# Row sums of 64 MB on one core: the first seven blocks' results get a store of their own

## Chip, cores, metric

One core of one Trainium2 chip. The metric is the device time of one execution in microseconds (us), lower is better. The kernel before takes 162.84 us (median of 3 runs, 162.84 to 163.09).

## The reference

```python
batch, seq, dim = 32, 512, 1024          # x: float32, 67.11 MB
def reference(x, multiplier):            # multiplier = 0.5
    return (np.sum(x, axis=-1) * multiplier).astype(np.float32)   # 16,384 results, 64 KB
```

## The kernel before

The 16,384 rows are laid over 128 partitions, 128 consecutive rows each. Eight blocks of 16 rows per partition (8 MB each) stream through three buffers. VectorE sums eight rows of a block in one instruction, ScalarE the other eight one by one. The last block arrives in five smaller pieces, so that little work is left after the last byte. All results collect in one tile, `res`, and leave in one store. All DMAs, loads and store, are issued by SyncE (SP), on one queue.

```python
x_rows = x_flat.rearrange("(p c) d -> p c d", p=P)
out_view = out.rearrange("b s -> (b s)").rearrange("(p c) -> p c", p=P)   # 128 rows of 512 B
...
for b in range(n_blocks - 1):                    # seven blocks of 8 MB
    t = x_pool.tile([P, B, D], fp32, name="xb")  # bufs=3
    loads.append(nc.sync.dma_start(out=t, in_=x_rows[:, c0 : c0 + B, :]))
    nc.vector.reduce_sum(...)                    # rows 0 to 7 of the block
    nc.vector.tensor_single_scalar(out=res[...], ...)   # times 0.5
    for r in range(h, B): act_row(t, r, c0 + r)  # rows 8 to 15
...
# last block: pieces of 8, 5, 2 rows, then row 15 in two parts (640 and 384 columns)
dve_span(t, B - 1, 0, cut, part)
dve_span(t, B - 1, cut, D, res[:, rows - 1 : rows], start=part)

seen = nc.sync.nop()                             # SP waits here for the loads and ScalarE
for i in loads[-8:] + acts[-1:]:
    tc.add_manual_dep(seen.ins, i.ins.name, ...)
store = nc.sync.dma_start(out=out_view, in_=res)
...
nc.at_finalize(start_loads_at_entry)  # moves the loads that wait for nothing (three) ahead of the entry barrier
```

## Time and profile before

| | before |
|---|---|
| time, median of 3 | 162.84 us |
| span of the profiled run | 161.1 us |
| read from HBM | 67.11 MB, 417 GB/s over the span |
| VectorE, ScalarE busy | 42% each |
| chain of waits | 86% loads, 11% VectorE |
| last VectorE work ends, last store issued, landed | 158.68, 158.78, about 160.3 us |

From the page of the kernel before: the span, the DMA engines' busy tenths in 40 equal slices (9 is 90% or more; a slice of 4.0 us holds only one or two of the blocks' 64 KB packets, which take 2.43 us each in the trace, and this is probably why 7 and 9 alternate), the queue's packets, megabytes and share of 16 engines' span, and the chain that ended last, by engine and then by line.

```profile
span 161.1 us, 233 instructions
...
DMA  7997997997997997997997998998998998999990
...
q1 hardware_dynamic: 1872, 67.18, 96.9%
...
DMA 86%; DVE 11%; SPq 1%; issue 0%; DVEq 0%
DMA xb<-in_x_dram 86%; DVE sums L76 11%; SPq L94 1%; DVE xb L60 1%; SPq L74 0%; DVE part L60 0%; DVEq L188 0%
...
```

The loads take 96.9% of all DMA time there is, and 86% of the chain. From the table of windows of the same kernel (stretch, its length, then each engine's busy time and instruction count, the clock, the DMA share and GB/s):

```profile
...
148.00:150.00 2.00, 1.61 (x5) 1.66 (x3) 0.00 (x0) 1.00 0.98 420
150.00:152.00 2.00, 0.92 (x4) 2.00 (x5) 0.00 (x0) 1.00 0.98 420
159.00:160.00 1.00, 0.00 (x0) 0.00 (x0) 0.00 (x0) 1.00 0.23 66
...
```

From 148 to 152 us the queue is full at 420 GB/s. Between 159 and 160 us only the store moves: 0.23 of that microsecond on the average engine. The timeline of the kernel before (start, duration, engine, line, operation, operands, and in brackets the idle time before it and what ended it), cut to VectorE's start on block seven and to the tail:

```profile
...
138.56 8.69 DVE L76 TENSOR_REDUCE sums<-xb 128x8 f32<-128x8192 f32 x1 [10.46 <-DMA xb<-in_x_dram]
...
157.68 0.49 DVE L60 CUSTOM_DVE_ANT_0 xb<-xb 128x320 f32<-128x320 f32 x1
...
158.26 0.42 DVE L60 CUSTOM_DVE_ANT_0 xb<-xb,part 128x192 f32<-128x192 f32 x1
...
158.78 0.35 SPq L123 DMA_DIRECT2D out_dram<-res  x1
```

The last row's first piece starts at 157.68, VectorE ends at 158.26 + 0.42 = 158.68, and SyncE issues the store 0.10 us later. The list of DMA issues of the same kernel (destination, source, queue, operation, count, size, us from issue to landing; the 192 KB are the last row's second part), and SyncE's waits after 145 us (who, for whom, us in total, times, longest):

```profile
...
xb<-in_x_dram SPq DMA_DIRECT2D x1, 192.0 KB, 47.6
...
out_dram<-res SPq DMA_DIRECT2D x1, 64.0 KB, 1.6
```

```profile
...
SPq L115 <- DMA xb<-in_x_dram: 38.9, 1, 38.9
SPq L188 <- DMA out_dram<-res: 1.2, 1, 1.2
...
```

The last load was issued at 110.49. The store needs 1.6 us to land; after it has landed there is only the exit. SyncE has nothing to do in most of the last 42 us: 38.9 us of them is one wait for loads.

### The profile page before, as it was taken

To read this page: it belongs to the slowest core of one execution; us is meant where nothing else is said; L and a number is where in the kernel's file an instruction comes from. 1 tells how busy PE (TensorE), PEld (TensorE's weight loads), DVE (VectorE), ACT (ScalarE), POOL (GpSimd) and SP (SyncE) were. 2 spreads that over 40 slices of the span, in tenths; PEclk is the share of its full clock that TensorE was granted. 3 is DMA by queue.
4 is the path that set the end of the run, shared out by engine and by line. 5 is a ranking of instruction groups with operands and counts; after the bars stand their busy time and mean duration, and the time that the engine had idled before them with its cause. 6 is when DMAs were issued, how large, how long until landed. Compare 5 with 4: busy or idle time off the path is not lost.

```text
span 161.1 us, 233 instructions
## 1 busy us (share of the span) xinstructions
DVE 68.1 (42%) x34; ACT 67.9 (42%) x127; POOL 0.2 (0%) x4
## 2 busy tenths in 40 slices
DVE  0000049700695008930099102990049700697453
ACT  3000049600694008920099001980039700596862
POOL 0000000000000000000000000000000000000000
DMA  7997997997997997997997998998998998999990
GB/s 260 521 456 325 521 456 325 521 456 325 521 456 325 521 456 325 521 439 342 521 439 344 521 423 358 521 423 358 521 407 374 521 407 374 415 439 411 423 381 30
DMA packets 1873, 67.18 MB, mean 417 GB/s; under 512 B 208, under 2 KB 464, under 8 KB 592
## 3 DMA queue, kind: packets, MB, share of 16 engines
q1 hardware_dynamic: 1872, 67.18, 96.9%
q14 instruction: 1, 0.01, 0.0%
HBM read 67.11 MB, written 0.07 MB: 417 GB/s over the span
## 4 chain that ended last, share of the span: by engine, by line
DMA 86%; DVE 11%; SPq 1%; issue 0%; DVEq 0%
DMA xb<-in_x_dram 86%; DVE sums L76 11%; SPq L94 1%; DVE xb L60 1%; SPq L74 0%; DVE part L60 0%; DVEq L188 0%
## 5 line engine op out<-in xcount | busy, mean ns | idle before, releaser
L50 ACT ACTIVATE xb<-xb 128x1024 f32<-128x1024 f32 x63 | 65.6, 1043 | 88.4 <-DMA xb<-in_x_dram 88.4
L76 DVE TENSOR_REDUCE sums<-xb 128x8 f32<-128x8192 f32 x7 | 60.8, 8686 | 85.2 <-DMA xb<-in_x_dram 85.2
L50 ACT ACTIVATION_READ_ACCUMULATOR xb<-xb 128x1 f32 x63 | 11.8, 187 | 0.0
L60 DVE CUSTOM_DVE_ANT_0 xb<-xb 128x512 f32<-128x512 f32 (+1 forms) x9 | 5.6, 667 | 5.1 <-DMA xb<-in_x_dram 4.9
L50 ACT ACT_TABLE_LOAD x1 | 1.3, 1283 | 1.7 <-PEq L174 1.7
L79 DVE TENSOR_SCALAR res<-sums 128x8 f32<-128x8 f32 x7 | 1.2, 172 | 0.2
L60 DVE DVE_READ_ACCUMULATOR2_ANT res<- 128x1 f32 x9 | 0.7, 82 | 0.0
L60 DVE CUSTOM_DVE_ANT_0 xb<-xb,part 128x192 f32<-128x192 f32 x1 | 0.4, 418 | 0.1
L174 POOL MEMSET const-bfloat16-1.0<- 128x1 bf16 x1 | 0.1, 101 | 0.0
L174 POOL MEMSET const-uint8-127<- 128x1 uint8 x1 | 0.1, 101 | 0.0
L174 POOL MEMSET const-float32-0.0<- 128x1 f32 x1 | 0.1, 98 | 0.2 <-issue 0.2
L174 POOL MEMSET const-float32-1.0<- 128x1 f32 x1 | 0.1, 98 | 0.0
L60 DVE DVE_READ_ACCUMULATOR2_ANT part<- 128x1 f32 x1 | 0.1, 81 | 0.0
## 6 DMA issues: line engine op xcount, KB each, us to landing
xb<-in_x_dram SPq DMA_DIRECT2D x1, 4096.0 KB, 39.6
xb<-in_x_dram SPq DMA_DIRECT2D x1, 2560.0 KB, 45.4
xb<-in_x_dram SPq DMA_DIRECT2D x1, 1024.0 KB, 47.4
xb<-in_x_dram SPq DMA_DIRECT2D x1, 320.0 KB, 47.7
xb<-in_x_dram SPq DMA_DIRECT2D x1, 192.0 KB, 47.6
xb<-in_x_dram SPq DMA_DIRECT2D x7, 49.3
out_dram<-res SPq DMA_DIRECT2D x1, 64.0 KB, 1.6
```

The lines of the kernel that those rows point to most:

```text
L50: acts.append(nc.scalar.activation(out=t[:, r, :], in_=t[:, r, :], func=mybir.ActivationFunctionType.Copy, scale=mul, accum_out=res[:, col ...
L60: nc.vector.tensor_tensor_reduce(out=t[:, r, lo:mid], in0=t[:, r, lo:mid], in1=t[:, r, mid:hi], scale=mul, scalar=start, op0=ADD, op1=ADD, ...
L76: nc.vector.reduce_sum(out=sums[:, c0 : c0 + h], in_=t[:, 0:h, :], axis=mybir.AxisListType.X)
L79: nc.vector.tensor_single_scalar(out=res[:, c0 : c0 + h], in_=sums[:, c0 : c0 + h], scalar=mul, op=mybir.AluOpType.mult,)
L94: nc.sync.dma_start(out=t[:, lo:hi, :], in_=x_rows[:, c0 + lo : c0 + hi, :])
L174: nc = _bacc.Bacc("TRN2", target_bir_lowering=False, num_devices=1)
```

## The change

Intent: most of the 64 KB of results are ready long before the end. Send them early, under the last loads, so that the store which stands on the critical path carries only the last block's 8 KB. The description of the change names also "three leading loads in front of the entry barrier"; the kernel before has that already, and the diff doesn't touch it. The built programs confirm it: both hold three loads ahead of the barrier.

```diff
@@ after the last load is issued
+    c1 = c0                                                        # 112 = 7 blocks x 16
+    nc.sync.dma_start(out=out_view[:, 0:c1], in_=res[:, 0:c1])     # 128 rows of 448 B
     on_act = {4, 5, 6, 7, 11, 12, 14}
...
-    store = nc.sync.dma_start(out=out_view, in_=res)               # 128 rows of 512 B
+    store = nc.sync.dma_start(out=out_view[:, c1:], in_=res[:, c1:])   # 128 rows of 64 B
```

What the diff doesn't show: the DMAs carry eight completion semaphores in turn (numbers 99, 100 and 103 to 108). With one more DMA ahead of it, the last store carries 106, which block six's load had, in place of 105. Of the loads' semaphores, SyncE's waits on the line of that store name 99 before, and 99, 100 and 106 after: one semaphore instruction more. It stands behind VectorE's last result.

## The prediction

> **What bounds it.** The loads. In the page's DMA line the 16 engines are 0.9 or busier in nearly every pair of slices and move 417 GB/s on average (67.11 MB read in a span of 161.1 us); the queue's packets take 96.9% of 16 engines' span. The chain of waits is 86% DMA xb<-in_x_dram. The table of windows gives 420 GB/s at a DMA share of 0.98 between 148 and 152 us, so no queue time is free before about 157 us.
>
> Outside the stream is the tail, from the timeline: last load seen at 157.65, two VectorE pieces (0.49 and 0.42 us) to 158.68, the store issued at 158.78 (0.35 us of SyncE), landing 1.6 us after issue, about 160.4, then some 0.7 us of exit barrier to 161.1.
>
> **What the change does.** The three leading loads already stand in front of the entry barrier in the kernel before and stay there; no load changes place. What is new is one store: 57,344 bytes of results (128 rows of 448 B) go out on the same SyncE queue after the last load was issued, and the final store shrinks from 64 KB to 8 KB (128 rows of 64 B). The early store waits for VectorE and ScalarE to finish block seven, at 147.45 us (timeline); SyncE is then idle (it waits 38.9 us for loads, in SyncE's list of waits). Its issue should cost about 0.35 us, as the old store's did, hidden.
>
> **Does it delay the loads?** It is queued at about 147.8 behind loads issued by 110.9. [...] This trace has no store in flight with loads. [...]
>
> **What it gains.** Bytes of the last store. The old store occupies 0.23 of the engines in one microsecond (159 to 160, table of windows), 0.23 us on average per engine. The new one has the same 128 rows, only shorter, so at most about 0.15 us of that goes, and the rest of the 1.6 us to landing is fixed. [...] The built program has also one more semaphore wait on SyncE before the final store (a few tens of ns), and the exit waits for two stores. The final store doesn't wait for the early one.
>
> **Sum.** -0.15 to +0.4 us on 162.84: 162.9 us. Range 162.5 to 163.5. Chances: faster by over 2% 0.01, within 2% 0.98, slower by over 2% 0.01.
>
> **What would show it.** Right: early store issued near 147.5 us on SyncE with about 10 us or more to landing; the last load still at 157.6 to 157.8; VectorE's end within 0.2 us of 158.68; final store to landing 1.4 to 1.9 us. Wrong: early store landing within 2 to 3 us (it overtook the loads); the last load later than 158; the final store over 2 us.
>
> **What would make it wrong.** [...] the small early packets share engines with the loads and delay the last one by a microsecond; or the exit waiting for the early store.

The sum came to -0.15 to +0.4 us, so 162.9 us. Two terms of it are cut above, because no trace showed them: a delay of the loads by the early store, and a loss with the shorter rows. They are what led up to +0.4. What is left of the sum is the gain of at most 0.15 us, the author's estimate from the 0.23 us in the table of windows, and the extra wait of a few tens of ns. The runs below measured 0.14 us for the one (the landing, 1.558 to 1.414 us) and 62 ns for the other (e2, e6).

## The result

| | before | after |
|---|---|---|
| median, same rounds | 162.88 us (6 runs, 162.78 to 163.21) | 162.81 us (6 runs, 162.63 to 163.12) |
| ratio after/before | | 0.9994, 95% interval 0.998 to 1.0007: same |

A ratio is the mean time of one kernel's fast runs over that of the other's in the same rounds, so it is not quite the ratio of the medians. Here it can't be told from 1. The profile shows what happened beneath that. The page of the changed kernel:

```profile
span 160.9 us, 236 instructions
...
DMA  7997997998998998998998998998998998999991
...
q1 hardware_dynamic: 2016, 67.18, 97.2%
...
DMA 86%; DVE 11%; SPq 1%; issue 0%; DVEq 0%
DMA xb<-in_x_dram 86%; DVE sums L76 11%; SPq L94 1%; DVE xb L60 1%; SPq L74 0%; DVE part L60 0%; DVEq L190 0%
...
```

The 0.2 us of span is not the change's: VectorE's start on block seven, before the early store exists, is already 0.21 us earlier (138.35 against 138.56) in the timeline of the changed kernel:

```profile
...
138.35 8.69 DVE L76 TENSOR_REDUCE sums<-xb 128x8 f32<-128x8192 f32 x1 [10.46 <-DMA xb<-in_x_dram]
...
147.31 0.35 SPq L105 DMA_DIRECT2D out_dram<-res  x1
...
157.46 0.49 DVE L60 CUSTOM_DVE_ANT_0 xb<-xb 128x320 f32<-128x320 f32 x1
...
158.04 0.42 DVE L60 CUSTOM_DVE_ANT_0 xb<-xb,part 128x192 f32<-128x192 f32 x1
...
158.62 0.34 SPq L125 DMA_DIRECT2D out_dram<-res  x1
```

The early store is issued at 147.31. From block seven's start to the start on the last row's first piece it is 157.46 - 138.35 = 19.11 us, against 157.68 - 138.56 = 19.12 before: the early store does not delay the load of that piece.

That load is not the last one, though the prediction and the expectations call it so (they took 157.65 us from the chain of waits). The last row's second part lands about 0.5 us later, at 158.1 us before and at 157.9 (110.31 + 47.6) after, and in all ten traces of this document VectorE starts on it 0.13 us after its landing, so it too sets the end. From block seven's start to the start on this part it is 158.26 - 138.56 = 19.70 us before and 158.04 - 138.35 = 19.69 after: no delay there either.

VectorE ends at 158.46, and now 0.16 us pass before the store is issued, not 0.10. The changed kernel's DMA issues and SyncE's waits:

```profile
...
xb<-in_x_dram SPq DMA_DIRECT2D x1, 192.0 KB, 47.6
...
out_dram<-res SPq DMA_DIRECT2D x1, 56.0 KB, 10.8
out_dram<-res SPq DMA_DIRECT2D x1, 8.0 KB, 1.4
```

```profile
...
SPq L105 <- DVE res L79: 36.5, 1, 36.5
SPq L117 <- DMA xb<-in_x_dram: 10.1, 1, 10.1
SPq L190 <- DMA out_dram<-res: 1.1, 1, 1.1
...
```

The early store lands 10.8 us after issue, at about 158.1, ahead of VectorE's end. The last store lands in 1.4 us, not 1.6. SyncE, which had only loads to wait for, now waits 36.5 us for the results of block seven (up to 147.31), issues the early store, and then waits 10.1 us for loads: the issue is hidden in idle time. The table of windows shows the shorter store:

```profile
...
148.00:150.00 2.00, 1.82 (x5) 1.86 (x3) 0.00 (x0) 1.00 1.02 440
150.00:152.00 2.00, 0.72 (x4) 2.00 (x5) 0.00 (x0) 1.00 0.91 389
159.00:160.00 1.00, 0.00 (x0) 0.00 (x0) 0.00 (x0) 1.00 0.09 8
...
```

Between 159 and 160 us the average engine is busy for 0.09 us, not 0.23. In the stretches before, 148 to 152, the mean rate is 414 GB/s ((440 + 389) / 2) against 420; the loads' packets of that stretch (20 KB, 0.76 us each in both traces) probably fall unevenly into windows of 2 us, and the 19.11 us above, which is the better measure, shows no loss.

**The sum.** The time of the profiled run less the moment when VectorE ends is 162.93 - 158.68 = 4.25 us before and 162.63 - 158.46 = 4.17 after. So the change is worth about 0.08 us in its only place, a shorter store less a longer way to it. Read from the trace to the nanosecond (it records the start, length and size of every DMA packet, too): the landing is 0.14 us shorter (1.558 to 1.414), the way to the issue 0.06 longer, and the exit after the landing 0.01 longer (0.80 to 0.81; all runs with two or more stores have 0.81, the three with one have 0.80). The first packet of the last store starts 0.84 to 0.85 us after the issue in both traces; moving the packets takes 0.36 us before and 0.21 after, so the whole gain lies in moving them. It is far below the scatter of the load stream (0.6 us between two traces of the changed kernel, e5).

### The profile page after: what moved, and what is told of

Its sections match the earlier page's. It is cut to its first block, busy times and chain, and to the rows that moved or that the text cites. A ratio compares the mean times of both kernels' runs of the same rounds, so it can differ in the third digit from the quotient of the medians.

```text
span 160.9 us, 236 instructions
## 1 busy us (share of the span) xinstructions
DVE 68.1 (42%) x34; ACT 67.8 (42%) x127; POOL 0.2 (0%) x4
## 4 chain that ended last, share of the span: by engine, by line
DMA 86%; DVE 11%; SPq 1%; issue 0%; DVEq 0%
DMA xb<-in_x_dram 86%; DVE sums L76 11%; SPq L94 1%; DVE xb L60 1%; SPq L74 0%; DVE part L60 0%; DVEq L190 0%
## 6 DMA issues: line engine op xcount, KB each, us to landing
xb<-in_x_dram SPq DMA_DIRECT2D x1, 192.0 KB, 47.6
out_dram<-res SPq DMA_DIRECT2D x1, 56.0 KB, 10.8
```

## Experiments

Two theories. *Tail*: the early store is free; the last store is 0.13 to 0.2 us shorter; the extra wait costs 0.06; nothing else changes. *Contention*: the gain is larger, but the early store's packets (or its small rows) delay the last loads and eat it. Each run leaves one trace. All traces are read for the same figures:

- **stream**: from VectorE's start on block seven to its start on the last row's first piece. A store that delays the loads up to that piece lengthens this.
- **to last part**: the same, to VectorE's start on the last row's second part, which the last load of all sets.
- **gap**: from VectorE's end to the issue of the last store.
- **landing**: from that issue to its landing.
- **tail**: the profiled run's time less VectorE's end.

All in us, taken from the nanoseconds of the traces and then rounded, so that the last digit can differ by one from a sum of printed lines:

| run | stream | to last part | gap | landing | tail | time of the profiled run | median, runs |
|---|---|---|---|---|---|---|---|
| before | 19.12 | 19.70 | 0.10 | 1.56 | 4.25 | 162.93 | 162.88, 6 |
| after | 19.11 | 19.70 | 0.16 | 1.41 | 4.17 | 162.63 | 162.81, 6 |
| e1: no early store | 19.12 | 19.69 | 0.10 | 1.43 | 4.12 | 162.88 | 162.93, 6 |
| e2: early store, full last store | 19.10 | 19.69 | 0.22 | 1.55 | 4.37 | 163.25 | 163.10, 5 |
| e3: early store from ScalarE | 19.23 | 19.81 | 0.16 | 1.42 | 4.18 | 163.06 | 162.98, 5 |
| e4: a store per block | 19.13 | 19.78 | 0.16 | 1.43 | 4.19 | 163.08 | 163.08, 5 |
| e5: changed kernel again | 19.13 | 19.70 | 0.16 | 1.41 | 4.17 | 163.26 | 162.89, 6 |
| e6: the extra wait moved | 19.10 | 19.69 | 0.10 | 1.41 | 4.11 | 162.98 | 162.91, 6 |
| e7: changed, loads not leading | 19.10 | 19.69 | 0.16 | 1.41 | 4.16 | 163.65 | 163.68, 6 |
| e8: before, loads not leading | 19.10 | 19.70 | 0.10 | 1.56 | 4.25 | 163.75 | 163.82, 5 |

The kernel before had a median of 162.89 us (11 runs) in the rounds of e1 to e4 and 162.95 (11 runs) in those of e5 to e8; the two sets of rounds ran on two different chips.

### e1: without the early store

```diff
-    nc.sync.dma_start(out=out_view[:, 0:c1], in_=res[:, 0:c1])
```

> The early store is left out, so seven blocks of results are never written: wrong on purpose. Tail theory (the early store costs nothing, the small last store gains 0.2 us, its extra wait loses 0.06): last load landing within the scatter of the two traces (157.4 to 157.7), VectorE's end to the store's issue back to 0.10 us from 0.16, landing 1.4 us after issue, 162.6 to 162.8 us. Contention theory (the early store delays the last loads and hides part of the gain): the last load lands 0.2 us or more earlier than with the early store and the time falls to 162.5 or less.

The result was wrong, as meant. Ratio to before 1.0002 (0.9987 to 1.0017). The timeline of this run:

```profile
...
138.65 8.69 DVE L76 TENSOR_REDUCE sums<-xb 128x8 f32<-128x8192 f32 x1 [10.46 <-DMA xb<-in_x_dram]
...
157.77 0.49 DVE L60 CUSTOM_DVE_ANT_0 xb<-xb 128x320 f32<-128x320 f32 x1
...
158.34 0.42 DVE L60 CUSTOM_DVE_ANT_0 xb<-xb,part 128x192 f32<-128x192 f32 x1
...
158.86 0.35 SPq L124 DMA_DIRECT2D out_dram<-res  x1
```

The stream is 157.77 - 138.65 = 19.12 us, no shorter than with the early store (19.11), and to the last part it is 19.69 (19.70 with it): contention is out. The tail is 4.12: the small store alone saves 0.13 us of 4.25, with the gap unchanged at 0.10, and the landing is 0.13 us shorter too (1.43 against 1.56). The last row's first piece started at 157.77, 0.31 later than with the early store, so the expectation's "within 157.4 to 157.7" missed: absolute times drift by more than that from run to run (0.62 us between the two traces of the changed kernel), differences within a trace don't (a stream of 19.10 to 19.13 us in nine of ten). The median, 162.93, is above the range expected, for the same reason.

### e2: early store kept, last store full again

```diff
-    store = nc.sync.dma_start(out=out_view[:, c1:], in_=res[:, c1:])
+    store = nc.sync.dma_start(out=out_view, in_=res)
```

> The early store stays, and the last store writes all 512 B rows again, as before; it now waits for the early one to land. Tail theory: landing back to 1.6 us after issue, two more waits than before ahead of the last issue (VectorE's end to issue about 0.2 us), time 162.9 to 163.1 us; the early store has landed by 158.2, before VectorE ends, so its wait adds nothing. Contention theory: last load after 157.9, time 163.2 or more.

Correct; ratio 1.0005 (0.9992 to 1.0018). The two stores overlap, so the last one waits for the early one, and two waits more than before stand ahead of the issue. The timeline of this run:

```profile
...
158.46 0.42 DVE L60 CUSTOM_DVE_ANT_0 xb<-xb,part 128x192 f32<-128x192 f32 x1
...
159.11 0.34 SPq L125 DMA_DIRECT2D out_dram<-res  x1
```

The gap is 159.11 - (158.46 + 0.42) = 0.23 us by the printed lines and 0.224 in nanoseconds, 0.12 more than before for two waits, so 0.06 each. The tail is 4.37, which is before's 4.25 plus that 0.12. The early store landed 10.8 us after its issue at 147.74, about 158.5, ahead of VectorE's end at 158.88, so it held nothing up. The stream is 19.10.

### e3: the early store on a queue of its own

```diff
-    nc.sync.dma_start(out=out_view[:, 0:c1], in_=res[:, 0:c1])
+    nc.scalar.dma_start(out=out_view[:, 0:c1], in_=res[:, 0:c1])
```

> The early store is issued by ScalarE, on its own queue. If the early store is free because it stands behind the loads in SyncE's queue, on its own queue it mixes with them: landing 2 to 4 us after issue and not 10.8, and its 0.22 us of engine time is paid by the loads, the last load up to 0.2 us later; ScalarE loses about 0.4 us before block eight, off the path. Time 162.8 to 163.2 us. Rival (the order in the queue doesn't matter, all stores wait for loads): landing stays near 10 us.

Correct; ratio 1.0003 (0.9991 to 1.0015). The DMA view of this run (queues with packets, megabytes and share; then the stores):

```profile
...
q1 hardware_dynamic: 1872, 67.12, 96.9%
q10 hardware_dynamic: 144, 0.06, 0.1%
...
out_dram<-res ACTq DMA_DIRECT2D x1, 56.0 KB, 8.2
out_dram<-res SPq DMA_DIRECT2D x1, 8.0 KB, 1.4
```

The store was issued at 147.64 and landed 8.2 us later, at 155.9; the last load landed at 158.3. So it moved among loads that were still to come, unlike on SyncE's queue (in the trace of the changed kernel its rows moved from 156.56 to 157.65, under the last pieces of the loads), and the stream is 0.11 to 0.12 us longer (19.23; all nine other traces have 19.10 to 19.13). But it took 8.2 us, not the 2 to 4 expected, an estimate that no trace had shown. The packet records of this trace show how it moved. The store has 144 packets, on average 9 for each of the 16 engines: 128 rows of 448 B, 25 ns each, and 16 packets of 4 B. They don't follow one another at once. The records don't name the engine, but two distances between the starts of these packets stand out, 0.327 us (74 pairs; its double has 51) and 0.779 us (51 pairs), and each is a little more than the time of one row, a single packet, of the loads then under way: 0.76 us for 20 KB in the second piece, 0.31 us for 8 KB in the third. The author reads this as single packets of the store between single packets of the loads. So the 8.2 us are 3.6 us to the store's first packet, at 151.25, then 4.2 us in which its packets are spread over the loads, to 155.49, and 0.4 us to landing. Why the first packet came so late is not shown; the last store, on a queue with nothing else in it, has its first packet after 0.85 us.

### e4: seven small early stores

```diff
+        if b >= 3:                       # in the block loop, after the load of block b
+            k0 = (b - 3) * B
+            nc.sync.dma_start(out=out_view[:, k0 : k0 + B], in_=res[:, k0 : k0 + B])
...
-    nc.sync.dma_start(out=out_view[:, 0:c1], in_=res[:, 0:c1])
+    for k in range(n_blocks - 1 - 3, n_blocks - 1):
+        nc.sync.dma_start(out=out_view[:, k * B : (k + 1) * B], in_=res[:, k * B : (k + 1) * B])
```

> Seven early stores of 64 B rows in place of one of 448 B rows; four of them stand in the queue between loads. The last store of this kind took 0.09 us per engine, so four among the loads should delay the stream by about 0.4 us (0.09 each): last load near 157.9, time 163.0 to 163.4 us. Rival (small packets slip into gaps and cost nothing anywhere): 162.8 us, last load 157.4 to 157.7. [...]

Correct; median 163.08, ratio 1.001 (0.9998 to 1.0022). Four stores of 64 B rows stand among the loads. The time is within the range of the first theory, which the scatter would also give without any cost, and a far larger cost of these stores (164 us or more) is out. The trace shows a small cost. Three of the four stores lie before VectorE's start on block seven, one in each stretch from block four on, and the fourth after it. From VectorE's start on block five to that on block six, and from six to seven, it is 19.39 and 19.38 us; the nine other traces have 19.34 to 19.37 in both. So a store cost 0.03 to 0.04 us there, under half of the 0.09 expected. (Before block five the stretches scatter by up to 0.3 us from trace to trace and hide it.) To the last part it is 19.78 us, 0.08 more than in any trace but e3's: the last load landed 0.53 us after the one before it, not 0.46 to 0.49, so VectorE's last part started 0.64 us after the first (158.47 - 157.83), 0.57 to 0.60 in the other nine. Why the last load was later is not shown, and all this is one trace.

### e5: the changed kernel again

No edit.

> The changed kernel once more. Tail theory (measured so far: last store 0.13 us shorter, its extra wait 0.05, nothing else): from VectorE's end to the end of the run 4.17 us (the run's time less VectorE's end), against 4.25 before; from VectorE's start on block seven to its start on the last row's first piece 19.11 us as before. The median then differs by 0.08 us from before, which the scatter of the load stream (0.3 us from run to run) hides: 162.6 to 163.1 us. Rival (the early store helps or hurts in some third place): one of the two stretches differs by more than 0.04 us.

Median 162.89, ratio 0.9999 (0.9987 to 1.0011). The tail is 4.17 again and the stream 19.13, though this trace came 0.63 us later overall. VectorE started on block seven at 138.97, not 138.35. The same kernel, twice: the load stream alone scatters by 0.6 us ahead of everything that the change touches.

### e6: the extra wait moved off the tail

The early store is made to wait also for block six's load, which has landed long before (VectorE starts on block six at 119.42 us in this trace, and the early store is issued at 147.72). With that the built program no longer has the extra wait after VectorE's end, as the count below shows.

```diff
-    nc.sync.dma_start(out=out_view[:, 0:c1], in_=res[:, 0:c1])
+    early = nc.sync.dma_start(out=out_view[:, 0:c1], in_=res[:, 0:c1])
+    tc.add_manual_dep(early.ins, loads[5].ins.name, ...Sync, DATA...)
```

> As the changed kernel, but the early store also waits for block six's load, long landed then, so the built program no longer needs that wait after VectorE's end. Tail theory: VectorE's end to the last store's issue 0.10 us in place of 0.16, end of VectorE to end of run 4.12 us (0.13 less than before), the two stretches otherwise as in the changed kernel; median 162.6 to 162.9 us. Rival (the gap ahead of the issue comes from something else than that wait): it stays at 0.16.

Correct; median 162.91, ratio 0.9996 (0.9983 to 1.0009). The timeline of this run:

```profile
...
158.45 0.42 DVE L60 CUSTOM_DVE_ANT_0 xb<-xb,part 128x192 f32<-128x192 f32 x1
...
158.97 0.34 SPq L131 DMA_DIRECT2D out_dram<-res  x1
```

The gap is 158.97 - (158.45 + 0.42) = 0.10 us and the tail 4.11: the wait was the cause of the 0.06. The waits can be counted in the traces, as SyncE's semaphore instructions on the line of the last store (line, operation, count, ns of one, first and last start), for the kernel before, the changed kernel, e2 and this run:

```profile
...
L123 SPq EVENT_SEMAPHORE  x1: 28/28/28, 158.7 to 158.7; - x1
...
L125 SPq EVENT_SEMAPHORE  x2: 28/28/28, 158.5 to 158.6; - x2
...
L125 SPq EVENT_SEMAPHORE  x3: 28/28/28, 158.9 to 159.0; - x3
...
L131 SPq EVENT_SEMAPHORE  x1: 28/28/28, 158.9 to 158.9; - x1
```

With 1, 2, 3 and 1 of them the gap is 0.100, 0.162, 0.224 and 0.100 us: 0.062 for each. In the trace this version has the shortest tail of all, 0.14 us less than before; in time it can't be told from either kernel.

### e7 and e8: the leading loads back behind the barrier

```diff
-    nc.at_finalize(start_loads_at_entry)
+    pass
```

> The changed kernel with the three leading loads left behind the entry barrier: the half of the description that the kernel before has already. The first load is then issued after the barrier and the whole stream starts later. ScalarE, which waits for the barrier, starts at 1.7 us in the trace of before, so estimate 1 to 1.7 us longer: 163.9 to 164.6 us. Rival (the barrier is over before the loads could start): no difference.

> The kernel before with the three leading loads behind the barrier. If the two halves of the description don't touch each other, this is as much slower than before as the other no-lead run is slower than the changed kernel: 1 to 1.7 us, and the two no-lead runs differ by 0.1 us at most. Rival (the early store matters more or less with the loads moved): they differ by 0.3 us or more.

e7 is the changed kernel so edited, e8 the kernel before. Medians 163.68 and 163.82, ratios to before 1.0045 (1.0032 to 1.0057) and 1.0052 (1.004 to 1.0064). So the other half of the description is worth 163.68 - 162.89 = 0.79 us with the early store and 163.82 - 162.95 = 0.87 us without, and it was in both kernels. The estimate of 1 to 1.7 us was too high. The start of the timeline of the kernel before, and then of e7, shows why:

```profile
...
0.00 1.32 SPq L74 DMA_DIRECT2D xb<-in_x_dram  x3
...
0.33 0.10 POOL L174 MEMSET const-uint8-127<- 128x1 uint8 x1
1.73 1.28 ACT L50 ACT_TABLE_LOAD   x1 [1.73 <-PEq L174]
```

```profile
...
0.33 0.10 POOL L176 MEMSET const-uint8-127<- 128x1 uint8 x1
0.73 1.28 ACT L50 ACT_TABLE_LOAD   x1 [0.73 <-PEq L176]
0.73 1.33 SPq L74 DMA_DIRECT2D xb<-in_x_dram  x3
```

Without leading loads the barrier ends at 0.73 us. The 1.73 us at which ScalarE starts in the kernel before, from which the estimate came, is late because SyncE first spends 1.32 us issuing three loads and only then comes to the barrier. The first load moves by 0.73 us, and the time by about as much. The two no-lead runs differ by 0.14 us, a little over the 0.1 expected; their tails (4.16 and 4.25) account for 0.08 to 0.09 of it, so the two halves don't touch each other as far as these runs can tell.

## Why the prediction was right

It forecast 162.9 us (162.5 to 163.5) and "within 2%"; 162.81 was measured, and 162.89 in the second set of rounds. This alone tests little: a range of 1 us around a change of 0.08 us would have held for almost any mechanism, and its sum leaned to slower (-0.15 to +0.4) where the tail got shorter. What speaks for the prediction is that the terms that stand agree one by one:

- *The loads bound the kernel and the change can only touch the tail*: right. 97% of DMA time before and after.
- *The early store stands behind the loads in the queue*: right, and it cost them nothing that can be measured. Streams of 19.11 and 19.13 us against 19.12, and without the early store 19.12; to the last part, which the last load of all sets, 19.70 and 19.70 against 19.70, and without the early store 19.69. e3 shows that this depends on the queue: on another queue 0.11 us. What the forecast assumed of the order within a queue was shown by no trace. Seen since: the store's rows moved from 156.56 to 157.65, the loads' until 157.48, and it landed 10.8 us after its issue, at 158.1, after the last load at 157.9.
- *A gain of at most 0.15 us from the shorter store*: right, 0.13 (e1) to 0.14 (the landing). The loss that the forecast allowed for shorter rows was not seen: 128 rows of 64 B landed 0.14 us sooner than 128 rows of 512 B. Per byte they were slower: in the packet records a row of 64 B took 10.4 ns and one of 512 B 27.0 ns, an eighth of the bytes in 0.39 of the time.
- *One more wait, a few tens of ns*: 0.06 us, shown by its removal (e6) and by two of them (e2). *The exit waits for two stores*: 0.01 us.
- *The sum, -0.15 to +0.4*: the tail changed by -0.13 + 0.06 = -0.07, read as 4.25 to 4.17.
- Two of the checks it offered were poorly chosen and narrowly failed: the last load "at 157.6 to 157.8" came at about 157.43 (the load of the last row's first part; the last of all was outside the check), and VectorE's end was 0.22, not 0.2, from 158.68. Both are absolute times in one trace, and e5 shows these moving by 0.6 us for one kernel. The difference within a trace was the right check.

Open: why the store of e3 waited 3.6 us for its first packet, and why the last load of e4 was 0.05 us late. The expectations drawn from single absolute times (e1) missed, as said.

## What to carry to other kernels

In this kernel, with 97% of all DMA time taken, splitting the final store paid 0.13 to 0.14 us of a 1.56 us landing; the rest was there for 8 KB as for 64 KB. Put an early store on the loads' own queue, after the last load, where it cost the loads nothing here (streams of 19.11 and 19.13 us against 19.12; 19.23 from a queue of its own), and look in the built program for waits that another DMA adds behind the last result (0.06 us each here). Judge effects below the run-to-run scatter by differences within a trace (end of compute to end of run), which repeated here within 0.02 us while whole runs of one kernel scattered by 0.6.
